# Gathering rows as quarters and transposing them on VectorE in a mixture-of-experts layer, with 128-row bias matmuls and a shorter SwiGLU

## The chip, the cores and the metric

One core of a Trainium2 chip runs the whole program. The metric is the device time of one execution in microseconds. The engines named below are TensorE (PE; its weight loads are PEld), VectorE (DVE), ScalarE (ACT), GpSimd (POOL) and SyncE (SP), which each execute their own instructions in program order and wait for one another through semaphores. Data moves between device memory and on-chip memory by DMA queues that SP, POOL and ACT feed.

## The reference, cut to what matters

A layer on 1024 tokens of width 1024: a mixer (short convolution and Fourier groups), cross-attention to 256 memory tokens, and a mixture of 32 experts of which each token takes 4. Nearly all of the time goes into the experts:

```python
def expert_block(args):                       # xb: 128 gathered rows of h, e: their expert
    xb, e = args
    gu = xb @ w_gate_up[e] + b_gate_up[e]     # 1024 -> 2 x 1024
    gate = jnp.minimum(gu[:, :D_EXPERT], SWIGLU_LIMIT)                 # 7.0
    up = jnp.clip(gu[:, D_EXPERT:], -SWIGLU_LIMIT, SWIGLU_LIMIT)
    glu = gate * jax.nn.sigmoid(SWIGLU_ALPHA * gate)                   # 1.702
    return ((up + 1.0) * glu) @ w_down[e] + b_down[e]
...
y = jnp.zeros((t + 1, d), out.dtype).at[row_tok].add(out * row_w[:, None].astype(out.dtype))
```

Everything is float32.

## The kernel before, in words

**Front.** The mixer, the attention and the router come first, up to about 617 us. The router writes the normed rows to `h_d` in device memory and a table `tab_d` of (row, weight) entries by expert. After that the 32 experts run one after the other until about 2040 us, and a short tail adds the residual and normalises.

**Experts.** `expert` (L1147) is called once per expert. An expert has 128 main rows; 17 of those called with a run-time index also have 32 remainder rows and are called heavy (H), the other 14 have none and are called light (L). Expert 0 of the order is fixed and has 64 remainder rows. The order is 0 1H 2H 3L 4H 5L 6H 7L 8H 9L 10H 11H 12L 13H 14L ... 21H 22H 23L ... 30H 31L: mostly heavy and light in turn, with three places where a heavy one follows a heavy one, and 13 where a heavy one follows a light one.

**Chunks and splits.** An expert's weights come as 12 chunks of 1 MB (`raw`), loaded by SP (`load_more`, L964). A chunk 128x2048 is split (`split`, L132) into a rounded high part `eh`, copied by ACT, and the rest `el`, subtracted by DVE, which waits for `eh`. `main_mm` (L1038) then does twelve matmuls of 128x512 per chunk: `eh` by the high part of the activations (L1062), `el` by the same (L1063), and `eh` by their low part (L1064). Chunks 0 to 7 are gate and up for two halves (c = 0, 1) of the hidden width, chunks 8 to 11 the down projection.

**Places.** The program order of each engine is written out by hand. An expert has 24 places: place 2j is in the middle of chunk j, place 2j+1 behind it. `place` (L1179) first does the work that is due there, then loads, then splits as many chunks ahead as a table says (`split_to`, L985; tables L43 to L48). What is due (tables L50 to L54): `glu_main` at places 7 and 15; `h_main(0)` and `h_main(1)`, the transposes and split of the SwiGLU result, at 13 and 17 (heavy) or 13 and 18 (light); `x_main` of the next expert, in two halves, at 19 and 21 (heavy) or 20 and 21 (light); `x_rem` of a next heavy expert at place 19. In a light expert, the first chunk of the next expert is split at place 18 or before, and the second chunk at place 21, behind both halves of `x_main`.

**Rows of x.** `prologue` (L925) runs when the first load of the next expert is issued, at place 11 of a heavy and place 3 of a light expert. SP loads the index table `idx`, and POOL gathers 128 rows of 4 KB from `h_d` into `xg` with one indirect DMA (L936); a heavy expert has the same for its 32 remainder rows (`idr`, `xgr`). `x_main` (L1018) takes four column blocks of 128x128 per half through PE transposes into PSUM (`transpose_split`, L1006; the transposes are L1009); ACT copies the high part `xthl` from there (L134), DVE subtracts the low one (L135). `x_rem` (L1024) does two small index operations on DVE (L1031, L1032), eight PE transposes of 32x32 rows (L1035) and one ACT copy into `xrt` (L1036). `rem_mm` (L1070) does the remainder's matmuls, 16 at a time, four side by side on 32 columns each; the first of a heavy expert stands four chunk-halves ahead of it.

**Bias and SwiGLU.** Each half of gate and up begins with one bias matmul for gate and one for up (L1049): a one-hot of 64 rows (`ohr`) against the table `BT`, whose upper 64 rows are gate's high and low part and lower 64 rows up's. The two run side by side on the upper and lower half of the array. `glu` (L998) is DVE min, ACT sigmoid, DVE clip, DVE multiply, DVE add-multiply on 128x512. `h_rem` (L1105) does the same on 128x128 for remainder rows. `bias_table` (L1234) builds `BT`, just ahead of expert 0.

Of the kernel before, what the change touches and what calls it, by code (L numbers as in the profile page):

```python
# [79 lines left out]
def kernel(ctx: ExitStack, tc: tile.TileContext, A, out, dbg=None):  # L80
# [804 lines left out]
    def tile_d(t):  # L885
        T = tiles[t]
        w, oh = T["w"], T["oh"]
        nc.vector.tensor_tensor(msum, msum, T["mk"], op=ALU.add)
        nc.vector.tensor_copy(msb, msum)
        sb = small("sb", [P, NE], bufs=2)  # L890
        nc.vector.tensor_tensor(sb, T["ps"][:, :NE], iote, op=ALU.add)
        nc.vector.tensor_tensor(oh, oh, sb[:, None, :].to_broadcast([P, 4, NE]), op=ALU.mult)
        nc.vector.tensor_reduce(w[:, 20:24], oh, axis=AX.X, op=ALU.add)
        sl = small("slot", [P, 4], I32, bufs=4)
        nc.vector.tensor_copy(sl, w[:, 20:24])
        pl = small("pl", [P, 4, 2], I32, bufs=4)
# [22 lines left out]
    st = [None] * NE  # L919
    ch = {}  # L920
    nload, nsplit = [0], [0]
    steps = []
    dead, pairs, slots = [0], [0], [SLOTS]

    def prologue(i):  # L925
# [17 lines left out]
    def tables(i):  # L943
        s = st[i]
        s["idx"] = small("idx", [P, 2], I32, bufs=3)
        nc.sync.dma_start(out=s["idx"], in_=tab_d[ds(s["e"] * ESTR, P), :])
        s["xg"] = s4("xg", [P, D])
        gather(s["xg"], h_d if i else h_d[:(EARLY + 1) * P], s["idx"], P)

    def rem_tables(i):  # L950
        s = st[i]
        m = s["m"]
        idr = s["idr"] = small("idr", [P, 2], I32, bufs=2)
        for g in range(2):
            nc.sync.dma_start(out=idr[g * m:(g + 1) * m], in_=tab_d[ds(s["e"] * ESTR + P, m), :])
        s["xgr"] = s4("xgr", [P, D])
        gather(s["xgr"], h_d, idr, m)
# [40 lines left out]
    def glu(hdst, pg, pu, n, m, tmp=None):  # L998
# [4 lines left out]
        nc.vector.tensor_tensor(g[:m, :n], g[:m, :n], sg[:m, :n], op=ALU.mult)  # L1003
        nc.vector.scalar_tensor_tensor(hdst, u[:m, :n], 1.0, g[:m, :n], op0=ALU.add, op1=ALU.mult)

    def transpose_split(src, dst, q, one=False):  # L1006
        tb = tp_bank()
        for j in range(4):
            nc.tensor.transpose(tb[:, j * P:(j + 1) * P], src(j), ident)  # L1009
        tv = tb.rearrange("p (a b) -> p a b", a=4)  # L1010
        if one and (one, q) in ON_DVE:
            nc.vector.tensor_copy(f(dst[:, 0, q * 4:q * 4 + 4, :]), tv)
        elif one:
            nc.scalar.activation(f(dst[:, 0, q * 4:q * 4 + 4, :]), tv, AF.Copy)
        else:
            split(tv, dst[:, 0, q * 4:q * 4 + 4, :], dst[:, 1, q * 4:q * 4 + 4, :])

    def x_main(i, q):  # L1018
        s = st[i]
        if q == 0:  # L1020
            s["xt"] = s8("xthl", [P, 2, KT, P], F32R)
        transpose_split(lambda j: s["xg"][:, (q * 4 + j) * P:(q * 4 + j + 1) * P], s["xt"], q, whole(12 * i) and 8 + i)

    def x_rem(i):  # L1024
        s = st[i]
        m = s["m"]
# [6 lines left out]
        tb = tp_bank()  # L1033
        for k in range(KT):
            nc.tensor.transpose(tb[:, k * m:(k + 1) * m], s["xgr"][:m, k * P:(k + 1) * P], ident[:m, :m])  # L1035
        nc.scalar.activation(xr, tb[:, :KT * m].rearrange("p (k t) -> p k t", k=KT), AF.Copy)  # L1036

    def main_mm(i, j, middle=None):  # L1038
        s = st[i]
# [2 lines left out]
        if g == 0 and j >= 8:  # L1042
            s[key] = mm_bank(key)
        elif g == 0 and t == 0:
            r = s["r"]
            for t in range(2):
                tsl = slice(t * 64, t * 64 + 64)
                b = s["gu"[t] + str(c)] = mm_bank(key)
                nc.tensor.matmul(b, ohr[tsl, r:r + 1].to_broadcast([64, P]), BT[0][tsl, hs[c]], start=True, stop=False)  # L1049
        raw, wh, wl = ch[12 * i + j][:3]  # L1050
        ps = s[key]
        if wh is None:
# [37 lines left out]
    def glu_main(i, c):  # L1090
        s = st[i]
        s[f"h{c}"] = t2("hh")
        glu(s[f"h{c}"], s[f"g{c}"], s[f"u{c}"], H2, P)

    def h_main(i, c):
        s = st[i]
# [8 lines left out]
    def h_rem(i, c):  # L1105

        s = st[i]
        m = s["m"]
        if c == 0:
            s["hr"] = s4("hrt", [P, KT, m])  # L1110
        tb = tp_bank()
        for j in range(4):
            nc.tensor.transpose(tb[:, j * P:(j + 1) * P], s[f"re{c}"][:, j * P:(j + 1) * P], ident)
        tv = s[f"re{c}"][:, :8 * m].rearrange("p (j t n) -> p j t n", j=4, t=2)
        tw = tb.rearrange("p (j u t n) -> p j u t n", j=4, u=64 // m, t=2)
        nc.vector.tensor_tensor(tv, tw[:, :, 0], s["bT"][:, c, :, :, None].to_broadcast([P, 4, 2, m]), op=ALU.add)
        if m == 32:
            nc.vector.tensor_tensor(tv, tv, tw[:, :, 1], op=ALU.add)
        a, b = (t2("ga").rearrange("p (a j n) -> p a j n", a=2, j=4)[:, :, :, :m] for _ in range(2))
        g, sg, u = a[:, 0], a[:, 1], b[:, 0]  # L1120
        nc.vector.tensor_scalar(g, tv[:, :, 0], LIMIT, None, op0=ALU.min)
        nc.scalar.activation(sg, g, AF.Sigmoid, scale=ALPHA)
        nc.vector.tensor_scalar(u, tv[:, :, 1], LIMIT, -LIMIT, op0=ALU.min, op1=ALU.max)
        nc.vector.tensor_tensor(g, g, sg, op=ALU.mult)
        nc.vector.scalar_tensor_tensor(s["hr"][:, c * 4:c * 4 + 4, :], u, 1.0, g, op0=ALU.add, op1=ALU.mult)
# [21 lines left out]
    def expert(i, hook=None, last=False):  # L1147
# [113 lines left out]
    def two_tiles(t, x2, c0):  # L1261
# [37 lines left out]
    tile_a(7, xD, H2 + HF)
# [5 lines left out]
    def count_order():  # L1305
# [93 lines left out]
    def beyond():  # L1399

        ordered.close()
        with tc.For_i(0, nblk, 1) as it:  # L1402
# [160 lines left out]
def layout(inputs):  # L1563
# [16 lines left out]
    gu = a["w_gate_up"][0].reshape(NE, 2, 4, P, 2, 2, H2).transpose(0, 5, 1, 4, 3, 2, 6).reshape(NE, 8, P, 4 * H2)  # L1580
# [25 lines left out]
```

## Time and profile before

| what | value |
|---|---|
| time, median of 3 runs | 2062.59 us (2059.86 to 2062.85) |
| the profiled execution | 2069.46 us, span 2067.6 us |
| mean granted TensorE clock | 0.994 of full speed |
| PE busy | 2028.4 us (98%), 10745 instructions |
| PEld busy | 1513.3 us (73%) |
| DVE busy | 1585.7 us (77%), 1991 instructions |
| ACT busy | 1122.3 us (54%), 1195 instructions |
| POOL busy | 227.3 us (11%), 190 instructions |
| DMA | 513.26 MB, mean 248 GB/s |

Busy time is summed per engine over the span. The profiled execution is 6.87 us above the median of the timed runs. In the expert part the page's slices show PE at nine tenths or more throughout, DVE at eight to nine, ACT at six to seven, and DMA at eight to nine.

### The profile page before, as it was taken

To read this page: it belongs to the slowest core of one execution; us is meant where nothing else is said; L and a number is where in the kernel's file an instruction comes from. 1 tells how busy PE (TensorE), PEld (TensorE's weight loads), DVE (VectorE), ACT (ScalarE), POOL (GpSimd) and SP (SyncE) were. 2 spreads that over 40 slices of the span, in tenths; PEclk is the share of its full clock that TensorE was granted. 3 is DMA by queue.
4 is the path that set the end of the run, shared out by engine and by line. 5 is a ranking of instruction groups with operands and counts; after the bars stand their busy time and mean duration, and the time that the engine had idled before them with its cause. 6 is when DMAs were issued, how large, how long until landed. Compare 5 with 4: busy or idle time off the path is not lost. (4 is left out here: it accounts for less than half of the span.)

```text
span 2067.6 us, 28604 instructions
## 1 busy us (share of the span) xinstructions
PE 2028.4 (98%) x10745; PEld 1513.3 (73%) x10745; DVE 1585.7 (77%) x1991; ACT 1122.3 (54%) x1195; POOL 227.3 (11%) x190
## 2 busy tenths in 40 slices
PE   8999999999999999999999999999999999999996
PEld 6888988888984567677776677676776676776764
DVE  6667668445576788888888798888988788888876
ACT  5233533334213566675666676666666576666754
POOL 0000100000133111010101111010111110110101
PEclk9999999999999999999999999999999999999999
DMA  4112434112358689898897998898998799898976
GB/s 156 47 62 72 133 125 161 31 42 86 107 192 302 231 286 358 302 318 321 310 363 254 333 320 323 306 362 302 318 327 304 283 339 320 306 348 298 332 301 249
DMA packets 104640, 513.26 MB, mean 248 GB/s; under 512 B 21298, under 2 KB 25651, under 8 KB 55347
## 3 DMA queue, kind: packets, MB, share of 16 engines
q1 hardware_dynamic: 83600, 445.87, 57.3%
q0 software_dynamic: 14080, 48.54, 9.4%
q10 hardware_dynamic: 6818, 16.99, 2.3%
q8 instruction: 86, 1.41, 0.3%
q14 instruction: 56, 0.45, 0.1%
HBM read 473.41 MB, written 37.95 MB: 247 GB/s over the span
## 5 line engine op out<-in xcount | busy, mean ns | idle before, releaser
L135 DVE TENSOR_TENSOR el<-raw,eh 128x2048 fp32r<-128x2048 f32 x372 | 831.0, 2287 | 121.3 <-ACT eh L134 119.8
L134 ACT ACTIVATE eh<-raw 128x2048 fp32r<-128x2048 f32 x372 | 690.6, 1908 | 7.1 <-PEq L1402 4.6
L1062 PE MATMUL g<-eh,xthl 128*128 128x512 f32 x992 | 401.2, 404 | 0.0
L1064 PE MATMUL g<-eh,xthl 128*128 128x512 f32 x992 | 388.1, 391 | 2.2 <-issue 2.2
L1063 PE MATMUL g<-el,xthl 128*128 128x512 f32 x992 | 388.5, 392 | 1.3 <-DVE el L135 1.3
L1062 PEld LDWEIGHTS g<-eh,xthl 128*128 128x128 f32 x992 | 186.5, 188 | 79.3 <-issue 39.7
L1064 PEld LDWEIGHTS g<-eh,xthl 128*128 128x128 f32 x992 | 186.6, 188 | 43.6 <-issue 2.6
L1063 PEld LDWEIGHTS g<-el,xthl 128*128 128x128 f32 x992 | 186.8, 188 | 36.9 <-DVE el L135 1.6
L1062 PE MATMUL d<-eh,hthl 128*128 128x512 f32 x496 | 205.9, 415 | 0.0
L1064 PE MATMUL d<-eh,hthl 128*128 128x512 f32 x496 | 195.1, 393 | 0.0
L1063 PE MATMUL d<-el,hthl 128*128 128x512 f32 x496 | 194.0, 391 | 0.0
L1085 PE MATMUL r<-raw,xrt 128*32 128x512 f32 (+1 forms) x1152 | 144.8, 598 | 0.7 <-ACT xrt L1036 0.7
L1001 ACT ACTIVATE sg<-g 128x512 f32<-128x512 f32 x64 | 40.4, 631 | 175.8 <-DVE g L1000 172.3
L940 POOL DMA_INDIRECT acc_d<-y,idx x31 | 74.4, 2400 | 393.1 <-ACT y L1131 296.4
L1062 PEld LDWEIGHTS d<-eh,hthl 128*128 128x128 f32 x496 | 93.2, 188 | 28.1 <-ACT xthl L134 10.9
L1064 PEld LDWEIGHTS d<-eh,hthl 128*128 128x128 f32 x496 | 93.1, 188 | 21.2
L1063 PEld LDWEIGHTS d<-el,hthl 128*128 128x128 f32 x496 | 93.6, 189 | 16.0
L134 ACT ACTIVATE hthl<-tp 128x512 fp32r<-128x512 f32 x62 | 37.1, 599 | 120.5 <-PE tp L1009 120.5
L145 PE MATMUL mm<-xh,wh 128*128 128x512 f32 x232 | 92.2, 397 | 6.0 <-ACT xh L137 6.0
L147 PE MATMUL mm<-xh,wl 128*128 128x512 f32 x232 | 91.0, 392 | 0.5 <-DVE wl L135 0.5
L146 PE MATMUL mm<-xl,wh 128*128 128x512 f32 x232 | 91.2, 393 | 0.0
L135 DVE TENSOR_TENSOR wl<-wraw,wh 128x1024 fp32r<-128x1024 f32 (+1 forms) x57 | 70.3, 1233 | 22.9 <-ACT wh L134 18.9
(377 smaller groups left out, 3243.0 us busy)
## 6 DMA issues: line engine op xcount, KB each, us to landing
raw<-in_w_exp SPq DMA_DIRECT2D x375, 1024.0 KB
raw<-in_w_exp POOLq DMA_DIRECT2D x9, 1024.0 KB
wraw<-in_w_in SPq DMA_DIRECT2D x15, 512.0 KB
xraw<-in_xT SPq DMA_DIRECT2D x16, 256.0 KB
wraw<-in_w_k SPq DMA_DIRECT2D x8, 512.0 KB
wraw<-in_w_v SPq DMA_DIRECT2D x8, 512.0 KB
wraw<-in_w_out SPq DMA_DIRECT2D x8, 512.0 KB
xres<-in_xT SPq DMA_DIRECT2D x16, 256.0 KB
```

Source lines behind the costliest of these rows:

```text
L134: nc.scalar.activation(dh, src, AF.Copy)
L135: nc.vector.tensor_tensor(dl, src, f(dh), op=ALU.subtract)
L145: nc.tensor.matmul(ps, lh, rh, start=start and i == 0, stop=False)
L146: nc.tensor.matmul(ps, lh, rl, start=False, stop=False)
L147: nc.tensor.matmul(ps, ll, rh, start=False, stop=stop and i == n - 1)
L940: nc.gpsimd.indirect_dma_start(out=dst, out_offset=bass.IndirectOffsetOnAxis(ap=idx, axis=0), in_=src, in_offset=None, compute_op=ALU.add)
L1001: nc.scalar.activation(sg[:m, :n], g[:m, :n], AF.Sigmoid, scale=ALPHA)
L1062: nc.tensor.matmul(ps, l[:, 0, kk, :], wh[:, k, :], start=j >= 8 and g == 0 and k == 0, stop=False)
L1063: nc.tensor.matmul(ps, l[:, 0, kk, :], wl[:, k, :], start=False, stop=False)
L1064: nc.tensor.matmul(ps, l[:, 1, kk, :], wh[:, k, :], start=False, stop=g == 1 and k == 3)
L1085: nc.tensor.matmul(ps[o:o + m], lhs[:, g * 4 + kk, :], ch[12 * i + j - 1 + t][0][:, kk, :], start=k == 0 and g == 0, stop=k == 4 // n - 1 ...
```

## The change

From expert 1 on, a row of `h_d` is no longer gathered whole. The row is seen as four quarters of 256 elements (1 KB), and quarter q of row t lands on partition 32q + t mod 32, so that four indirect DMAs of 128 quarters each fill `xg` for 128 rows, and one fills `xgr` for 32. Indices for that are loaded by four small SP DMAs (`iq`, `iqr`), and two DVE operations turn them into quarter numbers. These operations and the gathers are put GATHER = 2 places behind the place of the prologue. VectorE then transposes blocks of 32x32: one instruction of 128x512 for each half of `x_main`, reading with a step of eight elements and writing `xf`, from which ACT takes the high and DVE the low part; one of 128x256 straight into `xrt` for `x_rem`. PE transposes of x stay for expert 0 and in `beyond` (rows above what the static plan holds). The weight rows are reordered outside to match (feature p * 8 + k). The bias matmuls use all 128 rows with an `ohr` that is zero in the other half. The table holds up's bias plus one, `x_rem` adds one to the remainder's, and the SwiGLU becomes one ACT sigmoid that reads PSUM, and three DVE operations. `bias_table` moves from ahead of expert 0 into an earlier chunk of the attention's output projection.

```diff
@@ tables
-        s["xg"] = s4("xg", [P, D])
-        gather(s["xg"], h_d if i else h_d[:(EARLY + 1) * P], s["idx"], P)
+        if i:
+            s["iq"] = quarters("iq", s["e"] * ESTR, 4)
+            agenda.setdefault(now[0] + GATHER, []).append(lambda: gather_main(i))
+        else:
...
+    def quarters(name, base, n):
+        iq = small(name, [P, 4, 2], I32, bufs=2)
+        for i in range(4):
+            nc.sync.dma_start(out=iq[i * 32:(i + 1) * 32, :n], in_=tab_d[ds(base, n * 32), :].rearrange("(t a) c -> a t c", a=32))
+        return iq
+    def gather_quarters(x, iq, n):
+        nc.vector.tensor_copy(f(iq[:, :n, 1]), iq[:, :n, 0])
+        nc.vector.tensor_scalar(iq[:, :n, 0], f(iq[:, :n, 1]), 4.0, jd[:, 0:1], op0=ALU.mult, op1=ALU.add)
+        for t in range(n):
+            gather(x[:, t * HF:(t + 1) * HF], h_d.rearrange("r (i w) -> (r i) w", w=HF), iq[:, t, 0:1], P)
...
+    def swiglu(dst, g, u1, sg, u):
+        nc.scalar.activation(sg, g, AF.Sigmoid, scale=ALPHA)
+        nc.vector.tensor_scalar(u, u1, LIMIT + 1.0, 1.0 - LIMIT, op0=ALU.min, op1=ALU.max)
+        nc.vector.scalar_tensor_tensor(u, sg, SIGMOID_LIMIT, u, op0=ALU.min, op1=ALU.mult)
+        nc.vector.scalar_tensor_tensor(dst, g, LIMIT, u, op0=ALU.min, op1=ALU.mult)
@@ x_main
-        transpose_split(lambda j: s["xg"][:, (q * 4 + j) * P:(q * 4 + j + 1) * P], s["xt"], q, whole(12 * i) and 8 + i)
+        if i:
+            xf = t2("xf").rearrange("p (k t) -> p k t", k=4)
+            xq(s["xg"], xf, 4, slice(q * 4, q * 4 + 4))
+            split(xf, s["xt"][:, 0, q * 4:q * 4 + 4], s["xt"][:, 1, q * 4:q * 4 + 4])
...
+    def xq(x, dst, n, ks):
+        nc.vector.transpose(out=dst.rearrange("p k (t a) -> p k t a", a=32),
+                            in_=x[:, :n * HF].rearrange("p (t b k) -> p k t b", t=n, k=KT)[:, ks])
@@ x_rem
+        if i:
+            xq(s["xgr"], xr, m // 32, slice(0, KT))
...
+        nc.vector.tensor_scalar(s["bT"][:, :, :, 1], s["bT"][:, :, :, 1], 1.0, None, op0=ALU.add)
@@ main_mm
-                tsl = slice(t * 64, t * 64 + 64)
-                nc.tensor.matmul(b, ohr[tsl, r:r + 1].to_broadcast([64, P]), BT[0][tsl, hs[c]], start=True, stop=False)
+                nc.tensor.matmul(b, ohr[:, t, r:r + 1].to_broadcast([P, P]), BT[0][:, hs[c]], start=True, stop=False)
@@ glu_main
-        glu(s[f"h{c}"], s[f"g{c}"], s[f"u{c}"], H2, P)
+        swiglu(s[f"h{c}"], s[f"g{c}"], s[f"u{c}"], t2("sg"), t2("u"))
```

## Rows read from the trace of the kernel before

**Rows 1.** Windows: stretch, length, each engine's busy time, granted clock, DMA share, GB/s.
```profile
795.20:833.80 38.60, 38.60 (x191) 29.73 (x190) 34.51 (x26) 27.21 (x24) 4.80 (x4) 1.00 0.93 346
833.80:880.90 47.10, 47.10 (x258) 31.50 (x254) 38.76 (x38) 29.00 (x25) 4.11 (x3) 1.00 0.85 308
```

**Rows 2.** Groups by line and shape, PE: busy us, mean ns | idle before.
```profile
L1009 PE MATMUL tp<-cst,xg 128*128 128x128 f32 x256 | 38.5, 273 | 1.7 <-DMA xg<-h_d,idx 1.4 <-DVE re L1116 0.2
...
L1035 PE MATMUL tp<-cst,xgr 32*128 32x32 f32 x136 | 11.6, 224 | 0.0
```

**Rows 3.** Timeline of PE in a light expert: start us, duration us, instruction.
```profile
806.41 0.39 PE L1064 MATMUL g<-eh,xthl 128*128 128x512 f32 x1
806.73 0.50 PE L1049 MATMUL g<-BT,ohr 64*128 64x512 f32 x2
...
807.49 0.39 PE L1063 MATMUL g<-el,xthl 128*128 128x512 f32 x1
807.72 0.40 PE L1064 MATMUL g<-eh,xthl 128*128 128x512 f32 x1
...
824.34 0.40 PE L1064 MATMUL d<-eh,hthl 128*128 128x512 f32 x1
824.67 0.68 PE L1035 MATMUL tp<-cst,xgr 32*128 32x32 f32 x8
...
825.62 0.40 PE L1063 MATMUL d<-el,hthl 128*128 128x512 f32 x1
...
826.56 0.40 PE L1064 MATMUL d<-eh,hthl 128*128 128x512 f32 x1
826.80 0.60 PE L1009 MATMUL tp<-cst,xg 128*128 128x128 f32 x4
...
827.47 0.40 PE L1063 MATMUL d<-el,hthl 128*128 128x512 f32 x1
...
831.91 1.92 PE L1085 MATMUL r<-raw,xrt 128*32 128x512 f32 x16
...
837.28 0.39 PE L1063 MATMUL g<-el,xthl 128*128 128x512 f32 x1
```

**Rows 4.** Timeline of DVE, end of the same light expert and the next one's start.
```profile
825.81 4.50 DVE L135 TENSOR_TENSOR el<-raw,eh 128x2048 fp32r<-128x2048 f32 x2 [1.11 <-ACT eh L134]
...
830.40 0.15 DVE L1032 SCALAR_TENSOR_TENSOR ids<-idf,jd 64x1 int32<-64x1 f32 x1
830.47 1.27 DVE L135 TENSOR_TENSOR xthl<-tp,xthl 128x512 fp32r<-128x512 f32 x2
831.71 2.29 DVE L135 TENSOR_TENSOR el<-raw,eh 128x2048 fp32r<-128x2048 f32 x1
```

**Rows 5.** Timeline of ACT in the same stretch.
```profile
823.87 3.71 ACT L134 ACTIVATE eh<-raw 128x2048 fp32r<-128x2048 f32 x2
...
829.76 1.91 ACT L134 ACTIVATE eh<-raw 128x2048 fp32r<-128x2048 f32 x1
```

**Rows 6.** Groups by line and shape, DVE.
```profile
L1118 DVE TENSOR_TENSOR re<-re,tp 128x256 f32<-128x256 f32 x34 | 14.3, 421 | 1.2
...
L851 DVE TENSOR_REDUCE mk<-oh 128x32 f32<-128x128 f32 x8 | 3.1, 384 | 0.3
...
L535 DVE TENSOR_TENSOR yf<-pq 128x512 f32<-128x512 f32 x4 | 2.7, 686 | 0.0
...
L893 DVE TENSOR_REDUCE rt<-oh 128x4 f32<-128x128 f32 x8 | 2.3, 286 | 0.3
```

**Rows 7.** Groups by line and shape, ACT.
```profile
L134 ACT ACTIVATE wh<-wraw 128x512 fp32r<-128x512 f32 x2 | 1.3, 630 | 1.5 <-DMA wraw<-in_w_in 1.5
```

**Rows 8.** Timeline of POOL in the same light expert.
```profile
808.46 1.07 POOL L936 DMA_INDIRECT xg<-h_d,idx  x1 [4.97 <-DMA idx<-tab_d]
```

**Rows 9.** Timeline of PE: the first instruction after an idle stretch.
```profile
1972.12 0.50 PE L1064 MATMUL g<-eh,xthl 128*128 128x512 f32 x1 [2.16 <-issue]
```

**Rows 10.** Window of the same stretch, columns as in Rows 1.
```profile
1972.10:1976.00 3.90, 3.88 (x10) 3.05 (x11) 3.76 (x2) 2.40 (x3) 0.00 (x0) 0.56 0.96 399
```

More of the change, by code (lines that the diff above doesn't have):

```diff
@@ L30 @@
 ALPHA = 1.702
+SIGMOID_LIMIT = float(1.0 / (1.0 + np.exp(-ALPHA * LIMIT)))
 N64 = 0
@@ L49 @@
 AHEAD_LAST = (1, 4, 3, 5, 4, 4, 3, 2, 2, 5, 4, 5, 4, 4, 3, 4, 3, 4, 3, 5, 4, 5, 4, 5)
+GATHER = 2
 REM = (2, 4, 0, 4, 4, 1)
@@ L889, in tile_d @@
         nc.vector.tensor_copy(msb, msum)
-        sb = small("sb", [P, NE], bufs=2)
+        sb = small("sb", [P, NE])
         nc.vector.tensor_tensor(sb, T["ps"][:, :NE], iote, op=ALU.add)
@@ L921 @@
     nload, nsplit = [0], [0]
-    steps = []
+    steps, now = [], [0]
     dead, pairs, slots = [0], [0], [SLOTS]
@@ L946, in tables, with gather_main, gather_rem @@
         nc.sync.dma_start(out=s["idx"], in_=tab_d[ds(s["e"] * ESTR, P), :])
-        s["xg"] = s4("xg", [P, D])
-        gather(s["xg"], h_d if i else h_d[:(EARLY + 1) * P], s["idx"], P)
+        if i:
+            s["iq"] = quarters("iq", s["e"] * ESTR, 4)
+            agenda.setdefault(now[0] + GATHER, []).append(lambda: gather_main(i))
+        else:
+            s["xg"] = s4("xg", [P, D])
+            gather(s["xg"], h_d[:(EARLY + 1) * P], s["idx"], P)
+    def quarters(name, base, n):
[8 more added lines that the diff above has]
+            gather(x[:, t * HF:(t + 1) * HF], h_d.rearrange("r (i w) -> (r i) w", w=HF), iq[:, t, 0:1], P)
+    def gather_main(i):
+        st[i]["xg"] = s4("xg", [P, D])
+        gather_quarters(st[i]["xg"], st[i]["iq"], 4)
+    def gather_rem(i):
+        st[i]["xgr"] = s4("xgr", [P, H2])
+        gather_quarters(st[i]["xgr"], st[i]["iqr"], st[i]["m"] // 32)
     def rem_tables(i):
@@ L955, in rem_tables @@
             nc.sync.dma_start(out=idr[g * m:(g + 1) * m], in_=tab_d[ds(s["e"] * ESTR + P, m), :])
-        s["xgr"] = s4("xgr", [P, D])
-        gather(s["xgr"], h_d, idr, m)
+        if i:
+            s["iqr"] = quarters("iqr", s["e"] * ESTR + P, m // 32)
+            agenda.setdefault(now[0] + GATHER, []).append(lambda: gather_rem(i))
+        else:
+            s["xgr"] = s4("xgr", [P, D])
+            gather(s["xgr"], h_d, idr, m)
         s["bT"] = small("bT", [P, 2, 4, 2], bufs=2)
@@ L1021, in x_main, with feats @@
             s["xt"] = s8("xthl", [P, 2, KT, P], F32R)
-        transpose_split(lambda j: s["xg"][:, (q * 4 + j) * P:(q * 4 + j + 1) * P], s["xt"], q, whole(12 * i) and 8 + i)
+        if i:
+            xf = t2("xf").rearrange("p (k t) -> p k t", k=4)
+            xq(s["xg"], xf, 4, slice(q * 4, q * 4 + 4))
+            split(xf, s["xt"][:, 0, q * 4:q * 4 + 4], s["xt"][:, 1, q * 4:q * 4 + 4])
+        else:
+            transpose_split(lambda j: feats(s["xg"], P, q * 4 + j), s["xt"], q, 8)
+    def feats(x, m, k):
+        return x[:m].rearrange("p (f k) -> p k f", k=KT)[:, k]
+    def xq(x, dst, n, ks):
+        nc.vector.transpose(out=dst.rearrange("p k (t a) -> p k t a", a=32),
+                            in_=x[:, :n * HF].rearrange("p (t b k) -> p k t b", t=n, k=KT)[:, ks])
     def x_rem(i):
@@ L1032, in x_rem @@
         nc.vector.scalar_tensor_tensor(s["ids"][:n], idf[:n], 2.0, jd[:n, m // 64:m // 64 + 1], op0=ALU.mult, op1=ALU.add)
[L1033 to L1036, printed above, removed]
+        if i:
+            xq(s["xgr"], xr, m // 32, slice(0, KT))
+        else:
+            tb = tp_bank()
+            for k in range(KT):
+                nc.tensor.transpose(tb[:, k * m:(k + 1) * m], feats(s["xgr"], m, k), ident[:m, :m])
+            nc.scalar.activation(xr, tb[:, :KT * m].rearrange("p (k t) -> p k t", k=KT), AF.Copy)
+        nc.vector.tensor_scalar(s["bT"][:, :, :, 1], s["bT"][:, :, :, 1], 1.0, None, op0=ALU.add)
     def main_mm(i, j, middle=None):
@@ L1118, in h_rem @@
             nc.vector.tensor_tensor(tv, tv, tw[:, :, 1], op=ALU.add)
[L1119 to L1125, printed above, removed]
+        ab = t2("ga").rearrange("p (a j n) -> p a j n", a=2, j=4)
+        a, b = ab[:, 0, :, :m], ab[:, 1, :, :m]
+        swiglu(s["hr"][:, c * 4:c * 4 + 4, :], tv[:, :, 0], tv[:, :, 1], a, b)
     def y_main(i):
@@ L1179, in place @@
         def place(p):
+            now[0] = 24 * i + p
             for t in todo[p] + agenda.pop(24 * i + p, []):
@@ L1234, in bias_table @@
     def bias_table():
+        nc.vector.tensor_scalar(BT[1][64:], BT[1][64:], 1.0, None, op0=ALU.add)
+        for t in range(2):
+            o = slice(64 - 64 * t, 128 - 64 * t)
+            nc.vector.tensor_scalar(ohr[o, t, :], iot[o], 0.0, None, op0=ALU.mult)
+            nc.vector.tensor_copy(ohr[t * 64:t * 64 + 64, t, STATIC:STATIC + 1], eid[t * 64:t * 64 + 64, 4:5])
         nc.scalar.activation(BT[0], BT[1], AF.Copy)
@@ L1275 @@
     C[5].append((bias_load,))
+    ohr = small("ohr", [P, 2, NE], F32R)
     xC = x2_chunk(H2, places(*C))
@@ L1280 @@
         [(tile_r, xC), (tile_a, 4, xC, H2), (tile_b, 4)],
-        [(tile_o, 4)],
+        [(tile_o, 4), (bias_table,)],
         [(tile_c, 4), (tile_w, 4), (tile_d, 4)],
@@ L1289 @@
     dump("acc", acc_d)
-    ohr = small("ohr", [P, NE], F32R)
     ordr = small("ordr", [1, NE + 1], I32)
-    nc.vector.tensor_copy(ohr[:, STATIC:STATIC + 1], eid[:, 4:5])
     x_main(0, 0)
     tile_r(xD)
-    bias_table()
     x_main(0, 1)
@@ L1331, in ranks @@
             nc.vector.tensor_copy(ordr[:, 0:NE], ps[:1, 0:NE])
-            nc.vector.tensor_copy(ohr, R)
+            for t in range(2):
+                nc.vector.tensor_copy(ohr[t * 64:t * 64 + 64, t, :], R[t * 64:t * 64 + 64])
             ready[0] = True
@@ L1414, in beyond @@
                 for j in range(4):
-                    nc.tensor.transpose(tb[:, j * P:(j + 1) * P], x[:, (q * 4 + j) * P:(q * 4 + j + 1) * P], ident)
+                    nc.tensor.transpose(tb[:, j * P:(j + 1) * P], feats(x, P, q * 4 + j), ident)
                 nc.scalar.activation(xt[:, q * 4:q * 4 + 4, :], tb.rearrange("p (a b) -> p a b", a=4), AF.Copy)
@@ L1579, in layout @@
     o["w_o"] = _heads(a["w_o"][0]).transpose(1, 0, 2, 3, 4).reshape(8, P, 2, H2)
-    gu = a["w_gate_up"][0].reshape(NE, 2, 4, P, 2, 2, H2).transpose(0, 5, 1, 4, 3, 2, 6).reshape(NE, 8, P, 4 * H2)
+    gu = a["w_gate_up"][0].reshape(NE, P, KT, 2 * D).transpose(0, 2, 1, 3)
+    gu = gu.reshape(NE, 2, 4, P, 2, 2, H2).transpose(0, 5, 1, 4, 3, 2, 6).reshape(NE, 8, P, 4 * H2)
     dn = a["w_down"][0].reshape(NE, 2, 4, P, 2, H2).transpose(0, 1, 4, 3, 2, 5).reshape(NE, 4, P, 4 * H2)
```

## The prediction

> **What bounds the kernel now.** I read the page's busy times first, then windows over one light and one heavy expert, then the timelines of PE, DVE and ACT in them. In both windows PE's busy time is the whole length, 38.60 of 38.60 us and 47.10 of 47.10, at a granted clock of 1.00, while DVE has 34.51 and 38.76 us and the DMA share is 0.93 and 0.85 [rows 1]. So in the steady part every PE instruction taken away shortens the kernel, as long as the others stay ahead. But a light expert leaves DVE only 4.09 us and DMA 7% of its time. What a cut is worth depends on whether DVE's splits, ordered by hand, still come in time when PE is earlier. That is read at the end of a light expert, where DVE runs behind PE by several microseconds: the two `el` that place 18 orders end at 830.31, and what follows them goes gap by gap to the `el` that ends at 834.00 [rows 4]; PE takes the latter at 837.28 [rows 3], 3.28 us later. That is all the slack there.
>
> **What PE loses.** I take the start-to-start time across an operation, less that of the plain matmuls in it. Two plain neighbours, 807.49 and 807.72, are 0.23 us apart [rows 3].
>
> - Transposes of x: 826.56 to 827.47 is 0.91 us with four transposes and two plain steps, so 0.91 - 0.46 = 0.45 us for four [rows 3]. There are 256, in 64 fours [rows 2]; two fours of expert 0 stay. 62 x 0.45 = 27.9 us.
> - Transposes of remainder rows: 824.34 to 825.62 is 1.28 us; less 0.46 it is 0.82 us for eight [rows 3]. 136 are 17 x 8 [rows 2], and all go (expert 0 has a 64-row form): 13.9 us.
> - Bias: 806.41 to 807.72 is 1.31 us with three plain steps, so 0.62 us for the pair that runs side by side on 64 rows each [rows 3]. Two 128-row matmuls should cost two plain steps, 0.46 us; the price of a one-hot operand spread over 128 columns is that of the plain row, since the operand's shape is the same. 64 pairs, of which 17 follow the remainder's matmuls, where PE leaves the column groups anyway and I expect nothing: 47 x 0.16 = 7.5 us. Bounds: 0 if a 128-row pair is no cheaper than the one now, 10.2 us if all 64 save.
>
> Together 49.3 us of PE time. With every other engine in time, the profiled execution of 2069.46 us would come to 2020.2 and the median, 6.9 us below that execution, to about 2013. What PE idled in that execution (one stretch of 2.16 us and its half-clock sequel, [rows 9, 10]) is part of the 6.9.
>
> **What DVE and ACT gain and lose.** The shorter SwiGLU takes one DVE operation of 128x512 out of each half; it stands ahead of `h_main`, and DVE then waits for PE's transposes of the hidden rows anyway, so at the end of an expert nothing of it is left. Added in the tail is `xq`: no transpose by DVE is in the trace. The nearest row by size and by step is the 128x512 subtraction with reads in two places, 686 ns, and for 128x256 the 421 ns addition [rows 6]. I take 0.69 and 0.42 us. A lower bound is half of these, if a plain copy runs at twice that pace; an upper bound comes from the two reductions of 128 elements, 384 ns reading with a step and 286 ns without [rows 6]: 0.098 per 128 elements is 0.39 per 512, so 1.08 and 0.62 us.
>
> [...]
>
> Now the tail of a light expert before a heavy one, in DVE's order. Up to 830.31 nothing moves against PE, for it hangs on PE's transposes of the hidden rows, and these stay. Before: the index operations end at 830.55, both `xthl` subtractions at 831.74 (their high parts were long ready from PSUM), and `el` of the second chunk runs from 831.71 to 834.00 [rows 4], its `eh` having run at 829.76 to 831.67 on ACT [rows 5]. After:
>
> - 830.55 + 0.42 for the remainder's transpose = 830.97; the +1 on the small table 0.1 = 831.07;
> - `xf` first half 0.69, less 0.05 overlap (two in a row take 1.27, [rows 4]): 831.7; ACT's high part 0.63 [rows 7], 832.35; DVE's low part 0.69, 833.0;
> - `xf` second half 0.64: 833.65; ACT high part 0.63: 834.3;
> - only then ACT takes `eh` of the second chunk, for it stands behind in ACT's order: 3.71 / 2 = 1.86 [rows 5], 836.15; `el` 2.29 [rows 4]: 838.45.
>
> PE without a wait would be at that place at 837.28 - 0.82 - 2 x 0.45 = 835.56. It first waits at the remainder's matmuls, which would start at 831.91 - 1.72 = 830.19 [rows 3] and need `xrt` of 830.97: 0.78 us, so 836.34. Then it waits for `el` to 838.45, 2.1 us. Instead of 1.72 us earlier it is 1.17 later than before. What was PE work hidden from DVE is now a round trip DVE, ACT, DVE, twice, between two chunks that were just in time.
>
> **The sum.** A pair of a light and a heavy expert loses 4 x 0.45 + 0.82 + 3 x 0.16 = 3.10 us of PE; 1.72 of these stand in the light expert's tail and are lost, and 1.17 more: -3.10 + 1.72 + 1.17 = -0.2 us. 13 such changes: -3 us. At a heavy expert's end the first two chunks of the next are already split at place 17, so I expect no wait there; the three heavy ones before heavy ones give 0.82 + 0.90 + 0.48 = 2.2 us each, -6.6; what is left of the 49.3 us (49.3 - 13 x 3.10 - 6.6 = 2.4) comes too. Sum -12 us. `bias_table` and some operations are moved to the front's attention projection, about five DVE operations and one ACT copy; cover is the matmuls there, the price without it 3.5 us (five of 0.69), I take 1. 2069.5 - 12 + 1 = 2058.5 for the profiled execution, 2051.6 against the median: **2052 us**.
>
> **Gathers.** Now `idx` is waited for and the gather costs POOL 1.07 us [rows 8]. Four of the same and one more with 0.3 between are 6.9 us in a light expert, behind index operations of DVE at about 809, where DVE may wait up to 2 us for the indices, because their DMAs stand behind loads in SP's queue; cover is DVE's slack before place 18. The rows then land by some 820, ten microseconds before use. [...] Bytes are the same; added are some 600 packets of 8 B per expert.
>
> **Rivals.**
>
> *All of PE's saving comes* (DVE transposes are at the lower bound, or the low parts and splits overlap more than in my chain): with the waits gone 2013, with 0.8 us left at each of 13 changes 2023; 2013 to 2030. For it: PE is the bound in all windows. Against: slack was 3.28 us, and the chain eats 4.4.
>
> [...]
>
> *Strided reads cost:* 0.39 more on each `xf` and 0.2 on `xrt`, 1.0 us later at each of 13 changes: 2065.
>
> *Rows come late* in heavy experts, by 2 us at 15 places: 2080.
>
> **How the numbers follow.** The chain as worked out, 2042 to 2062: 0.45. All of PE's saving: 0.20. Clock: 0.20. Strided reads: 0.10. Late rows: 0.05. A measurement can tell 0.2%, 4 us: faster is below 2058.5, slower above 2066.7. Faster has the first rival and most of the forecast, 0.20 + 0.38; same has the rest of the forecast and most of the strided case, 0.15; slower 0.27. Range 2022 to 2077, the forecast's own being 2042 to 2062.
>
> **What would show it.** PE matmul groups L1009 of `xg` at 8 left and 32x32 ones gone; bias as 128 rows at the plain 0.23 us spacing. In light experts' tails PE idle before the L1063 of the second chunk, released by DVE's `el`, near 2.1 us, and before the remainder's first matmuls 0.8, released by DVE's transpose; DVE transposes near 0.69 and 0.42 us. Wrong if PE stays busy through the change to a heavy expert, if the clock falls after these waits, or if POOL's gathers release DVE's transposes.

## The result and the profile after

The changed kernel takes 2129.84 us (median of 4 runs, 2122.32 to 2135.57) against 2062.72 us before (4 runs too, one more than in the table above): ratio 1.0315, 95% interval 1.0286 to 1.0343, so 3.2% slower. The prediction was 2052 us with a range up to 2077. The profiled execution has a span of 2123.1 us, 55.5 more than before.

Busy times of the changed kernel, from the page:

```profile
PE 2012.3 (95%) x10361; PEld 1499.7 (71%) x10361; DVE 1636.6 (77%) x2089; ACT 1110.1 (52%) x1178; POOL 333.5 (16%) x283
```

PE has lost work (2028.4 us before), and its share fell from 98% to 95%: it now idles. The windows of a light and the following heavy expert, which answer to [rows 1]:

```profile
983.89:1022.88 38.99, 37.24 (x173) 28.57 (x172) 34.09 (x31) 25.18 (x20) 11.89 (x7) 1.00 0.93 347
1022.88:1073.43 50.55, 48.03 (x249) 32.09 (x245) 42.48 (x40) 30.29 (x27) 6.23 (x5) 0.97 0.75 278
```

The light expert is 0.39 us longer than the 38.60 before although PE works 1.36 us less, and the heavy one is 3.45 us longer; there the mean granted clock is 0.97. Over the whole run the 13 light experts in front of a heavy one take 38.82 to 40.72 us each (38.59 before). PE's waits from expert 1 on (engine, line, who ended them: us in total, times, longest):

```profile
PE g L1118 <- DVE el L137: 23.7, 13, 1.8
PE d L1119 <- DVE hthl L137: 13.2, 13, 1.1
PE g L1117 <- ACT eh L136: 9.1, 13, 0.8
PE d L1118 <- DVE el L137: 6.1, 13, 0.5
PE tp L1048 <- DVE hh L1043: 3.6, 6, 1.5
PE r L1140 <- DVE bT L1092: 3.0, 14, 0.2
PE g L1119 <- issue: 2.2, 1, 2.2
```

The first six lines are 58.7 us; the kernel before has the last of the seven and, of the other kinds, a single wait of 1.3 us like the first. The first and third are the wait before the second chunk of a heavy expert, at 13 places as forecast. The second and fourth lie in the light experts and were not forecast. The fifth lies in six of these, those where DVE waits for an index load:

```profile
DVE iqr L965 <- DMA iqr<-tab_d: 5.2, 6, 1.7
```

The tail of the light expert on DVE, which answers to [rows 4]:

```profile
1015.67 4.49 DVE L137 TENSOR_TENSOR el<-raw,eh 128x2048 fp32r<-128x2048 f32 x2 [1.11 <-ACT eh L136]
1020.08 0.14 DVE L1083 CAST idf<-idr 64x1 f32<-64x1 int32 x1
1020.25 0.15 DVE L1084 SCALAR_TENSOR_TENSOR ids<-idf,jd 64x1 int32<-64x1 f32 x1
1020.33 0.64 DVE L1073 STREAM_TRANSPOSE xrt<-xgr 128x256 f32<-128x256 f32 x1
1020.90 0.12 DVE L1092 TENSOR_SCALAR bT<-bT 128x8 f32<-128x8 f32 x1
1020.94 1.10 DVE L1073 STREAM_TRANSPOSE xf<-xg 128x512 f32<-128x512 f32 x1
1022.74 0.69 DVE L137 TENSOR_TENSOR xthl<-xf,xthl 128x512 fp32r<-128x512 f32 x1 [0.69 <-ACT xthl L136]
1023.35 1.15 DVE L1073 STREAM_TRANSPOSE xf<-xg 128x512 f32<-128x512 f32 x1
1025.20 0.69 DVE L137 TENSOR_TENSOR xthl<-xf,xthl 128x512 fp32r<-128x512 f32 x1 [0.70 <-ACT xthl L136]
1027.00 2.29 DVE L137 TENSOR_TENSOR el<-raw,eh 128x2048 fp32r<-128x2048 f32 x1 [1.11 <-ACT eh L136]
```

Between the end of the index operations (1020.40) and the `el` of the second chunk lie 6.6 us, of which DVE works some 4.1 and waits 2.5, in three round trips to ACT (0.69, 0.70, 1.11). PE in the same stretch:

```profile
1021.03 1.92 PE L1140 MATMUL r<-raw,xrt 128*32 128x512 f32 x16 [0.22 <-DVE bT L1092]
...
1027.02 0.49 PE L1117 MATMUL g<-eh,xthl 128*128 128x512 f32 x1 [0.69 <-ACT eh L136]
1029.35 0.50 PE L1118 MATMUL g<-el,xthl 128*128 128x512 f32 x1 [1.83 <-DVE el L137]
...
1030.22 0.63 PE L1118 MATMUL g<-el,xthl 128*128 128x512 f32 x1
1030.65 0.63 PE L1119 MATMUL g<-eh,xthl 128*128 128x512 f32 x1
```

PE waits 0.69 us for `eh` and 1.83 us for `el`; 0.9 us later its matmuls are 0.43 us apart instead of 0.23: the granted clock is 0.50 from 1030.2 to 1033.5. Windows of 8 us that begin 6 us into each of the 13 heavy experts behind a light one show a clock under 1.00 in ten of them (nine at 0.79, one at 0.59), and 1.00 in three; the first, and one of the three:

```profile
849.00:857.00 8.00, 7.57 (x34) 4.75 (x35) 7.34 (x5) 8.00 (x5) 1.85 (x1) 0.79 0.75 201
...
1754.50:1762.50 8.00, 7.44 (x39) 4.77 (x40) 7.34 (x5) 8.00 (x5) 1.99 (x1) 1.00 0.79 213
```

Last, expert 0 is some 12 us longer. Its one long wait, in PE's and then in DVE's list of waits for 624 to 717 us: PE waits for index operations that stand, in DVE's order, behind a transpose, and this transpose waits for the gathered rows.

```profile
PE rd L1140 <- DVE idf L1083: 11.8, 1, 11.8
```
```profile
DVE xf L1073 <- DMA xg<-h_d,iq: 10.2, 1, 10.2
```

### The profile page after: what moved, and what is told of

Read it like the earlier page. It is cut to its first block, busy times and chain, and to the rows that moved or that the text cites. A ratio compares the mean times of both kernels' runs of the same rounds, so it can differ in the third digit from the quotient of the medians.

```text
span 2123.1 us, 28914 instructions
## 1 busy us (share of the span) xinstructions
PE 2012.3 (95%) x10361; PEld 1499.7 (71%) x10361; DVE 1636.6 (77%) x2089; ACT 1110.1 (52%) x1178; POOL 333.5 (16%) x283
## 5 line engine op out<-in xcount | busy, mean ns | idle before, releaser
L1118 PE MATMUL g<-el,xthl 128*128 128x512 f32 x992 | 396.1, 399 | 23.7 <-DVE el L137 23.7
L1117 PE MATMUL g<-eh,xthl 128*128 128x512 f32 x992 | 400.6, 404 | 11.8 <-ACT eh L136 9.1
L1117 PEld LDWEIGHTS g<-eh,xthl 128*128 128x128 f32 x992 | 189.5, 191 | 85.3 <-ACT eh L136 23.8
L938 POOL DMA_INDIRECT xg<-h_d,iq x124 | 146.5, 1181 | 576.0 <-DVE iq L966 286.9
L1119 PEld LDWEIGHTS g<-eh,xthl 128*128 128x128 f32 x992 | 190.4, 192 | 44.5 <-issue 2.6
L1119 PE MATMUL d<-eh,hthl 128*128 128x512 f32 x496 | 195.7, 394 | 13.2 <-DVE hthl L137 13.2
L1117 PE MATMUL d<-eh,hthl 128*128 128x512 f32 x496 | 200.4, 404 | 0.0
L136 ACT ACTIVATE xthl<-xf 128x512 fp32r<-128x512 f32 x62 | 39.2, 632 | 172.0 <-DVE xf L1073 172.0
L1040 ACT ACTIVATE ga<-re 128x128 f32<-128x128 f32 (+1 forms) x36 | 11.4, 317 | 200.9 <-DVE re L1173 194.5
```

Of the source, the lines that this page charges most:

```text
L136: nc.scalar.activation(dh, src, AF.Copy)
L938: nc.gpsimd.indirect_dma_start(out=dst[:m], out_offset=None, in_=src[:, :], in_offset=bass.IndirectOffsetOnAxis(ap=idx[:m, 0:1], axis=0))
L1117: nc.tensor.matmul(ps, l[:, 0, kk, :], wh[:, k, :], start=j >= 8 and g == 0 and k == 0, stop=False)
L1118: nc.tensor.matmul(ps, l[:, 0, kk, :], wl[:, k, :], start=False, stop=False)
L1119: nc.tensor.matmul(ps, l[:, 1, kk, :], wh[:, k, :], start=False, stop=g == 1 and k == 3)
```

## The experiments

Times are medians; ratios are against the kernel before in runs on the same chip.

**Bias alone (e1).** The kernel before with

```diff
-                nc.tensor.matmul(b, ohr[tsl, r:r + 1].to_broadcast([64, P]), BT[0][tsl, hs[c]], start=True, stop=False)
+                nc.tensor.matmul(b, ohr[:, t, r:r + 1].to_broadcast([P, P]), BT[0][:, hs[c]], start=True, stop=False)
```

> The kernel before with the 128-row bias matmuls alone (one-hot zero-padded to 128 rows); gather, transposes, SwiGLU and table as before. Theory: PE is the bound before, and the 47 pairs that stand between plain matmuls each drop from 0.62 to about 0.46 us, so 6 to 8 us less: 2055 to 2057 us. Rival: the pair of 128-row matmuls costs as much as two half-array matmuls side by side: 2062 us, no change.

Measured 2056.22 us, ratio 0.9962 (0.9949 to 0.9975), 8.2 us less. The term of the sum (7.5 us) holds. It is spread otherwise than forecast: a light expert takes 38.34 us (0.26 less, forecast 0.32) and a heavy one 46.85 (0.25 less, forecast 0.16), so the pairs behind the remainder's matmuls gain too.

**x back on PE (e2, e9).** The changed kernel with whole-row gathers and PE transposes; e9 also has the old order of the weight rows.

```diff
-            xq(s["xg"], xf, 4, slice(q * 4, q * 4 + 4))
-            split(xf, s["xt"][:, 0, q * 4:q * 4 + 4], s["xt"][:, 1, q * 4:q * 4 + 4])
+        transpose_split(lambda j: feats(s["xg"], P, q * 4 + j), s["xt"], q, i == 0 and 8)
```

> The changed kernel with x gathered in whole rows again and transposed by PE (reading with a step of eight elements); bias, SwiGLU and the moved bias table stay changed. Theory: all of the slowdown comes from the gather and the transposes on VectorE, so what stays is the bias gain: 2053 to 2060 us. Rival: the shorter SwiGLU, with ScalarE reading PSUM, or the earlier bias table take part in the slowdown: above 2070 us. No x transpose on VectorE, no wait before the second chunk of a heavy expert, no half-clock stretch behind it.

> The kernel with x on PE again, the bias and the SwiGLU changed, and now also the old order of the weight rows, so that PE's transposes take 128 (or 32-row) blocks of adjacent elements. Theory: the 7 us between this kernel with a step of eight (2063) and the bias alone (2056) are PE's eight remainder transposes with operands read in steps, 0.4 us at each of 17 experts; without the step: 2054 to 2058. Rival: the SwiGLU or the moved bias table cost these 7 us: 2061 to 2065.

e2 took 2063.43 us (1.0005, 0.9994 to 1.0016), 3 us above its theory's upper end and below its rival; e9 took 2055.92 us (0.9958, 0.9944 to 0.9972), as its theory said. So all of the slowdown is in the gather and the transposes on DVE; beside e1 (0.9962) no cost or gain of the SwiGLU and the bias table shows. e2's 7 us are PE's remainder transposes reading with a step of eight; their group in e2, then in e9, 6.6 us apart:

```profile
L1074 PE MATMUL tp<-cst,xgr 32*128 32x32 f32 x136 | 18.1, 272 | 0.0
```
```profile
L1074 PE MATMUL tp<-cst,xgr 32*128 32x32 f32 x136 | 11.5, 224 | 3.9 <-DMA xgr<-h_d,idr 3.9
```

**The reading step (e3).** Another order of the weight rows lets DVE read 32 adjacent elements; expert 0 gets an ACT copy for it.

```diff
-                            in_=x[:, :n * HF].rearrange("p (t b k) -> p k t b", t=n, k=KT)[:, ks])
+                            in_=x[:, :n * HF].rearrange("p (t k b) -> p k t b", t=n, k=KT)[:, ks])
```

> The changed kernel with another order of the weight rows (feature = 256 * (p // 32) + 32 * k + p % 32), so that VectorE's transposes read 32 elements in a row; expert 0 gets one more ScalarE copy for it. Theory: the step of eight costs 0.46 of the 1.15 us of a transpose; without it the transposes are 0.69 and 0.42 us, the second chunk's el of a heavy expert comes about 1.15 us earlier, PE's wait of 1.83 us falls to about 0.7, and the granted clock stays at full: 13 x (1.15 + 1.7) = 37 us less, and about one more in each light expert: 2080 to 2095 us. Rival A: the clock falls all the same, 13 x 1.15 = 15 us less: 2110 to 2120. Rival B: the price is the transpose's own and not the reading step's: transposes stay at 1.15 us, time 2125 to 2135.

2104.43 us, 1.0200 (1.0182 to 1.0218): 25 us less than the changed kernel, between the theory's number and rival A's. The price of the step is as said; DVE's groups, of the changed kernel and of e3:

```profile
L1073 DVE STREAM_TRANSPOSE xf<-xg 128x512 f32<-128x512 f32 x62 | 71.4, 1152 | 10.3 <-DMA xg<-h_d,iq 10.2
...
L1073 DVE STREAM_TRANSPOSE xrt<-xgr 128x256 f32<-128x256 f32 x17 | 11.0, 646 | 0.0
```
```profile
L1079 DVE STREAM_TRANSPOSE xf<-xg 128x512 f32<-128x512 f32 x62 | 43.4, 699 | 12.7 <-DMA xg<-h_d,iq 12.7
L1079 DVE STREAM_TRANSPOSE xrt<-xgr 128x256 f32<-128x256 f32 x17 | 7.3, 429 | 0.0
```

But the wait at the second chunk fell only by the 0.69 us for `eh`; the 1.8 us for `el` stayed (from the list of waits of e3 for 990 to 1034 us):

```profile
PE g L1125 <- DVE el L137: 1.8, 1, 1.8
```

`el` starts when `eh` ends and takes 2.29 us, and `eh` still came just as PE asked for it (it ends at 1029.03, PE takes it at 1029.10), PE being earlier too. Seven of the 13 windows of 8 us still have a lower clock, 0.79 to 0.81. Shorter transposes alone do not change that `eh` stands behind x. Of its own, e3 lost some 10 us more in expert 0 than the changed kernel (95.87 us against 85.72), where PE's weight loads waited 7.4 us for ACT's copy.

**The second chunk earlier (e4).** One number of AHEAD_LIGHT, place 20: 3 becomes 4.

> The changed kernel with one number changed: in a light expert the second chunk of the next expert is split at place 20, behind the first half of x_main, and not at place 21 behind both. Theory: the second chunk's eh hung on ScalarE behind the high part of the second half; now it runs 2.4 us earlier, and PE's waits of 0.69 and 1.83 us fall to under 0.5 with no fall of the clock behind them: 13 x (2.1 + 1.5) = 47 us less, about 2083 us (2075 to 2095). Rival: the second half of x comes late for the third chunk instead, the wait moves there, and the time stays within 10 us of 2130.

2130.41 us, 1.0324 (1.0303 to 1.0345). The rival was right: the wait only moved. PE's waits from 720 to 1920 us:

```profile
PE g L1118 <- DVE el L137: 23.6, 22, 1.8
PE d L1119 <- DVE hthl L137: 15.8, 16, 1.1
```

It is now 0.3 us at the second chunk and 1.8 at the third, whose `eh` stands behind the second half of x.

**Fewer round trips (e5).** Same operations, in this order at one place:

```diff
+            ahead_of = eh_only(12 * i + 2)        # eh of the next chunk, ScalarE
+            for h in range(2):
+                xq(s["xg"], xfs[h], 4, slice(h * 4, h * 4 + 4))
+            for h in range(2):
+                nc.scalar.activation(s["xt"][:, 0, h * 4:h * 4 + 4], xfs[h], AF.Copy)
+            for h in range(2):
+                nc.vector.tensor_tensor(s["xt"][:, 1, h * 4:h * 4 + 4], xfs[h], f(s["xt"][:, 0, h * 4:h * 4 + 4]), op=ALU.subtract)
+                if not h:
+                    ahead_of()                    # its el
```

> The changed kernel with x_main in another order: both transposes of VectorE first, then ScalarE's two high parts, then VectorE's low parts; the eh of the next weight chunk stands ahead of the high parts on ScalarE, its el between the two low parts on VectorE. The same operations, all at the place of the first half. Theory (round trips, not work, make the waits): VectorE's three idle stretches of 0.7, 0.7 and 1.1 us at each expert's end go, the second chunk's el comes about 2.8 us earlier, PE's waits of 0.69 and 1.83 us and the half clock behind them go at 13 places (13 x 4 = 52 us), and those of 1.07 and 0.48 us in light experts mostly go (10 to 20 us); expert 0's wait stays: 2060 to 2080 us. Rival A (VectorE has too much work, whatever its order): waits move to the next split, 2110 us or more. Rival B: the second chunk is cured and the light experts' waits stay: 2080 to 2090.

2088.52 us, 1.0113 (1.0090 to 1.0136): 41 us less, rival B. The light and the heavy expert:

```profile
988.03:1027.05 39.02, 37.24 (x173) 28.56 (x171) 33.75 (x31) 24.84 (x20) 11.65 (x7) 1.00 0.90 337
1027.05:1072.96 45.91, 45.91 (x248) 31.16 (x245) 42.15 (x40) 30.50 (x27) 6.62 (x5) 1.00 0.85 314
```

The heavy one has no wait, a clock of 1.00, and is 1.19 us shorter than the 47.10 before, with the slow transposes still in it. The light one keeps its waits; and where a heavy expert follows a heavy one, `xrt` now comes behind both halves of x, a new wait of 3.0 us at three places. In three light experts, where DVE waits 1.7 to 2.1 us for an index load, PE waits another 1.9 to 2.2 us.

**Indices on POOL (e6).** The two index operations by GpSimd, the gathers at once:

```diff
-            agenda.setdefault(now[0] + GATHER, []).append(lambda: gather_main(i))
+            gather_main(i)
...
-        nc.vector.tensor_copy(f(iq[:, :n, 1]), iq[:, :n, 0])
+        nc.gpsimd.tensor_copy(f(iq[:, :n, 1]), iq[:, :n, 0])
```

> The changed kernel with the two index operations done by GpSimd in place of VectorE, and the gathers issued right behind the index loads instead of two places later. Theory: in expert 0 the gather for expert 1 starts some 10 us earlier, so the wait of 11.8 us for xg and the half clock behind it go (12 + 5 us); in light experts VectorE has 0.9 us less ahead of the SwiGLU and waits for no index load, so the 1.07 us waits shrink: 8 to 14 us. Waits before the second chunk stay. 2100 to 2112 us. Rival: the gather's place is not what makes expert 0 late (the queue of the index loads is): 2120 to 2130.

2103.85 us, 1.0200 (1.0178 to 1.0221), as the theory said; its two edits were not run apart. In expert 0 the wait of 11.8 us is 0.9:

```profile
PE rd L1140 <- DVE idf L1083: 0.9, 1, 0.9
```

and the light experts' 1.07 us are at most 0.3 (line 4 of PE's waits from 720 to 1920 us):

```profile
PE g L1118 <- DVE el L137: 21.9, 12, 1.8
PE g L1117 <- ACT eh L136: 8.6, 12, 0.8
PE d L1118 <- DVE el L137: 5.5, 12, 0.5
PE d L1119 <- DVE hthl L137: 3.1, 12, 0.3
```

**A wait by itself (e11).** The kernel before, with eight unused subtractions on DVE ahead of the second chunk's `el`:

```diff
+        if q and i > 1 and s["m"] and not st[i - 1]["m"]:
+            late = t2("late")
+            for _ in range(8):
+                nc.vector.tensor_tensor(late, s["xg"][:, :H2], s["xg"][:, H2:], op=ALU.subtract)
```

> The kernel before with nothing of the change, and eight more subtractions of 128x512 on VectorE (their result is not used) between the low part of x's second half and the second chunk's el, at the 13 places where a heavy expert follows a light one. They take 8 x 0.64 = 5.1 us, and the slack there was 3.28. Theory: PE waits 1.8 us at the L1063 of the second chunk, 13 x 1.8 = 24 us, and behind some or all of these waits the granted clock is half for 3.4 us, 1.5 us lost each, 10 to 20 us: 2095 to 2108 us. Rival A: the half clock in the changed kernel came from something else (its DMAs, its gathers), not from the wait: 2085 to 2090, no half clock. Rival B: the slack is larger than read: under 2075.

2113.16 us, 1.0217 (1.0200 to 1.0234); 45 us more, above the theory's upper end, for the wait is 2.27 us (1.8 expected). Two heavy experts of this run:

```profile
925.16:974.85 49.69, 47.42 (x256) 31.44 (x252) 44.04 (x44) 28.59 (x25) 3.86 (x3) 1.00 0.79 291
1013.49:1064.72 51.23, 48.96 (x256) 32.57 (x252) 44.21 (x44) 28.90 (x25) 3.39 (x3) 0.97 0.78 283
```

Both have the same wait; the first is 2.59 us longer than the 47.10 before, the second 1.54 more, with a clock of 0.97. Seven of 13 had a lower clock (0.79 or 0.80 in windows of 8 us, 1.00 in the other six). So a wait at this place is enough, with none of the change's DMAs or transposes: it costs its length, 0.3 us for the start, and 1.5 us where the clock falls.

**All cures (e7, e8, e10).** e7 joins e3, e5 and e6, and moves the write of the overflow list to SP's queue. e8 adds two edits, e10 only the first of them:

```diff
+            due = agenda.pop(24 * i + p, [])
+            for t in due + todo[p] if p == x0 else todo[p] + due:      # x_rem ahead of x_main
...
-AHEAD_LIGHT = (..., 3, 1, 4, 1, 3, 4, 2, 2)
+AHEAD_LIGHT = (..., 3, 4, 4, 1, 3, 4, 2, 2)
```

> All cures together: contiguous transposes (other order of the weight rows), x_main with transposes first and the next eh ahead, index operations on GpSimd with the gather at once, and the write of the overflow list moved from ScalarE's to SyncE's queue. Theory: no PE wait of over 0.3 us is left between light and heavy experts and none over 1 us in expert 0, the clock stays at full, and PE's saving of some 45 to 49 us comes through: 2015 to 2035 us, under the kernel before. Rival: VectorE stays the bound of a light expert's tail: 2050 to 2070 us.

> The kernel with all cures and two more: where a heavy expert follows a heavy one, the remainder's rows are transposed ahead of x_main and not behind it, and in a light expert chunk 11 is split one place earlier (17 instead of 18). Theory: the waits of 2.10 us at three places (with half clock behind two of them) and of 0.46 us in 14 light experts go: 3 x 2.1 + 2 x 1.5 + 14 x 0.46 = 16 us less than with all cures, 2024 to 2032 us. Rival: the earlier split delays the high part of the hidden rows on ScalarE, and PE waits there instead: 2035 to 2045.

> All cures and the remainder's rows transposed ahead of x_main where a heavy expert follows a heavy one; chunk 11 of a light expert is split at place 18 again. Theory: the earlier split at place 17 had turned a wait of 0.46 us into one of 0.91 in 14 light experts (37.49 us became 37.83); back at 18 this is 14 x 0.34 = 4.8 us less than the kernel with both edits (2033.5): 2026 to 2031 us. Rival: the length of a light expert was made by something else than that split: 2032 to 2036.

e7 2041.87 us, 0.9894 (0.9872 to 0.9915), between the theory and its rival: three waits of 2.1 us where heavy follows heavy, and 0.46 in each light expert. e8 2033.52 us, 0.9859 (0.9839 to 0.9880), again between the two: the first waits are gone, but the earlier split turned the 0.46 into 0.9 at the next operation:

```profile
PE d L1151 <- DVE hthl L137: 11.7, 13, 0.9
```

e10 2032.33 us, 0.9832 (0.9818 to 0.9845), on a chip on which the kernel before took 2068.04: 1.7% faster than before. The time lies in the rival's range (2032 to 2036), 1.2 us below e8. By ratio it gains 0.27 points, some 5 us, but the two intervals touch and the chips differ. The traces show the theory's saving where it was expected: a light expert takes 37.47 us, in e8 37.80. All that is left in its experts from 720 to 1920 us:

```profile
PE d L1150 <- DVE el L137: 5.5, 12, 0.5
PE r L1172 <- DVE bT L1124: 0.5, 1, 0.5
```

## Why the prediction was wrong

The sign was wrong; the place of the main wait was right. Of the 55.5 us between the two profiled executions, 12.4 are in expert 0 and 45.9 between the start of the first light expert and the start of the last one; experts 1 and 2 are 2.8 us shorter. By the steps of the prediction:

- **What PE loses** held. e1 gave 8.2 us for the bias (7.5). In e10 a light expert's PE work is 37.47 - 0.46 = 37.01 us and a heavy one's 45.91, against 38.60 and 47.10: 2.78 us a pair (3.10 forecast). The stretch of 2.16 us that was put down to the 6.9 us stands in the other profiled executions too (2.18 in the changed kernel, 2.2 in e9), so it is hardly what made that one slower.
- **What DVE and ACT gain and lose** named the wait before the second chunk, 13 times, behind a round trip DVE, ACT, DVE. Its size: 0.78 + 2.1 us forecast, 0.22 + 0.69 + 1.83 measured. But the net of such a pair was put at -0.2 us and is +3.84 in the windows shown: waits of 1.75 us in the light and 2.52 in the heavy expert, 1.5 for the clock, less the 2.78 saved; the rest, 0.85, is what PE loses as it starts again behind these waits (an estimate by difference; e11 shows 0.3 for one). So these failed:
  - *The transposes' price.* 0.69 and 0.42 us were taken, 1.152 and 0.646 measured, above the upper bounds of 1.08 and 0.62 too. The row that decided, 686 ns for reads in two places, was the wrong neighbour, since each of its reads ran over adjacent elements by itself. The two reductions came nearer. The lower bound was an estimate whose pace no row shows: the one copy of 128x512 on DVE before takes 692 ns (L1012, from PSUM). e3 shows that the step of eight is what costs: 699 and 429 ns without it; no run tries another step.
  - *The clock.* It had a chance of 0.20 and no place in the sum, though it stands once in the trace of before: 0.56 over 3.9 us, behind an idle stretch of 2.16 us [rows 9, 10]. In the changed kernel it falls behind ten of 13 waits (0.79 or 0.59 in windows of 8 us), and e11 prices it at 1.5 us each, with no cause but a wait.
  - *"Up to 830.31 nothing moves against PE."* It does, from both sides. PE comes to chunk 11's `el` sooner, because the transposes of x that stood ahead of it are gone, while the chain that makes this `el` keeps its length: `el` starts 3.06 us behind PE's transposes of the hidden rows before ([rows 4]) and 3.07 after. PE took it 6.55 us behind them; now it is there after some 5 and waits. The first two lines are of the kernel before, the others of the changed one:

```profile
822.75 0.60 PE L1009 MATMUL tp<-cst,hh 128*128 128x128 f32 x4
...
829.30 0.39 PE L1063 MATMUL d<-el,hthl 128*128 128x512 f32 x1
```
```profile
1012.60 0.60 PE L1048 MATMUL tp<-cst,hh 128*128 128x128 f32 x4
...
1018.02 0.50 PE L1118 MATMUL d<-el,hthl 128*128 128x512 f32 x1 [0.46 <-DVE el L137]
```

This wait of 0.46 to 0.51 us, 13 times, is not late work of DVE: it stands unchanged in e10, with all cures. The other wait in light experts, up to 1.07 us, is. Round trips in the heavy expert's tail put the first `el` of the light one 3.5 us behind its start (before, 0.16), and index operations stand ahead of the SwiGLU, which starts 17.7 us into the expert (before, 13.4). DVE's lines before and after:

```profile
795.36 13.30 DVE L135 TENSOR_TENSOR el<-raw,eh 128x2048 fp32r<-128x2048 f32 x6 [1.11 <-ACT eh L134]
808.58 0.68 DVE L1000 TENSOR_SCALAR g<-g 128x512 f32<-128x512 f32 x1
```
```profile
987.39 13.40 DVE L137 TENSOR_TENSOR el<-raw,eh 128x2048 fp32r<-128x2048 f32 x6 [1.11 <-ACT eh L136]
...
1001.56 0.68 DVE L1041 TENSOR_SCALAR u<-g 128x512 f32<-128x512 f32 x1
```

DVE then reaches `h_main` late. Without the index operations on DVE (e6) at most 0.3 of the 1.07 us is left; with the other order alone (e5) 1.08 stays, since DVE there waits 2.60 us for ACT's `eh` in place of the round trips. "At a heavy expert's end I expect no wait" looked at PE only and not at what DVE carries into the next expert.

- **Gathers** were followed in light experts and not in expert 0, where GATHER puts the index operations at place 17 and x is due at 18: 11.8 us, and a granted clock of 0.64 in the 4.2 us behind it. In e6 the first gather starts 40.5 us into expert 0 (at 659.18) instead of 58.4 (at 682.36), and 0.9 us of the wait is left. Rows land 6.3 us behind a gather's issue (median of the changed kernel's 124). The cover named for late indices, DVE's slack before place 18, was not there in six light experts: DVE waits up to 1.7 us for them, and PE up to 1.5 behind it.
- **How the numbers follow** treated clock, strided reads and late rows as alternatives. The clock and the strided reads came together, at the same places: the step makes the wait longer, and without it (e3) the clock falls in seven of 13 places (0.79 to 0.81) instead of ten. Late rows came in expert 0 alone, and not at the 15 places of that rival. In us: e3, e5 and e6 give back 25, 41 and 26, together 93, and all cures together 88 (e7).

## What to carry to other kernels

Work moved from the bound engine to one that is idle a tenth of the time is free only if no other engine must answer within it: count the round trips in program order, not the busy share, and put the first parts of all chains ahead of the second parts (e5: 41 us for the same operations in another order). Where a chain behind the bound engine keeps its length, making that engine faster uses up the slack there by itself (here 0.46 us of wait, 13 times). When a rival's mechanism would lengthen the wait that another rival needs, give their joint case a chance of its own. An access with a step is priced from a row with the same step (here 1152 ns with the step of eight, 699 without).

## What the runs showed beside

- A wait for `el` right behind a wait for `eh` is 1.82 or 1.83 us at all 13 places: about the 2.29 us of the subtraction, less PE's matmul in between (0.49). In e3, where PE no longer waits for `eh`, and in e4, where the wait stands one chunk later, it keeps this size.
- In expert 0, ACT's issue of a small write (the overflow list) stood waiting for index loads of SP and held the SwiGLU behind it: in e4's list for 645 to 692 us, `ACT sg` waits 12.1 us for `iq`, in the changed kernel 6.2. PE then waited 5.1 to 5.7 us at the remainder (e4, e5, e6) or 0.7 (the profiled execution). In e7, with the write in SP's queue, it is 0.7, and ACT's wait for `iq` is gone; with e5's or e6's edits alone it stays.
